# A pair's outputs turned one unit later, and the gate of the modulation made in an earlier phase

## The chip, the cores and the metric

The kernel runs on one core of a Trainium2 chip. The metric is the device time of one execution in microseconds (us); before the change its median is 1662.65 us over three runs. TensorE does the matrix products and the transposes, VectorE (DVE in the rows) and ScalarE (ACT) the elementwise work, GpSimd (POOL) small helpers and some transfers, and SyncE (SP) issues most loads. [...]

## The reference

One block of a hybrid network on 256 tokens `x` and 256 context tokens `ctx` of width 2048, in float32. What matters here:

```python
mod = jax.nn.silu(c) @ w_ada[l] + b_ada[l]            # 2048 -> 3 * 2048
shift, scale, gate = jnp.split(mod[:, None, :], 3, axis=-1)
xn = rmsnorm(h, norm_gain[l]) * (1.0 + scale) + shift  # cn: the context, with c_ctx
aq, ak, av, ag, hq, hff, hfb, hi, hg, ma, mb = split_columns(xn @ w_in[l])
caq, cak, cav, cag, chq, chff, chfb, chi, chg, cma, cmb = split_columns(cn @ w_in[l])
# window attention with rotary positions and a sink, over tokens and context -> att_branch
# f = lb + (1 - lb) * sigmoid(z): a scan in both directions over 16 heads of 128, its start
# state from the context -> o; o is normalised and gated -> hg_branch
y = sigmoid(ma + b[0]) * (hg_branch @ w_o_hgrn) + sigmoid(mb + b[1]) * (att_branch @ w_o_attn)
h = h + gate * (y @ w_out)
return rmsnorm(h, final_norm_gain)
```

`shift` and `scale` are needed at the very start. `gate`, the last third of the modulation (a row vector of 2048 values from a 2048 x 2048 piece of `w_ada`), is needed only at the very end.

## The kernel before

A float32 product is made of three products of split halves: each chunk of weights (128 x 1024) is loaded into a buffer `raw` (a rotation of four), ScalarE rounds it to the high half `wh` (L76, L577), and VectorE takes the difference as the low half `wl` (L77, L578). `wh` and `wl` have three buffers each. The stages in order of time, by the span of the profiled execution:

- To about 130 us: `x` and `ctx` are turned and normalised, `shift` and `scale` are made, and the first products with `w_in` run.
- To about 560 us: the forget gates and values of the scan, by a scheme with seven block products in place of eight (`quad_col`, 13 calls of seven steps; `quad_tok`, three calls of twice seven steps). VectorE also makes the weights' sums and differences (`combos`, L558). `bank8` deals out all eight PSUM banks in turn, among them those named `tp` and `o`. Results go to DRAM from the buffers F0.
- To about 1083 us: eight pairs of heads (`pair`), each a generator with small work on all engines. `weave` mixes it with a filler (`inputs`): the remaining projections of `w_in`, in chunks. A pair yields the amount of filler that it wants next, in units (STEP) of 24 matmuls of 512 columns; a filler chunk is half a unit, or a whole one where four blocks of tokens are projected.
- From about 1100 us: the output products `part_a` with `w_o_hgrn`, the attention, `part_b` with `w_o_attn`, then `w_out` and the last norm.

TensorE's order within the seven-product phase and within the pairs is that of the program (`manual_schedule`); that of the other engines and queues, and of TensorE's work outside such blocks, is set by the framework's planner, which runs its own model of time when the program is built, takes what is ready, and prefers what has a raised priority (`high_priority`: the splits `wh` and `wl`, the `combos`), and else what comes first in the program.

A pair does, in order: the scans that make the decays `E` (L741, L742, L745, in the buffer X2, which also holds the former pair's score tiles AT and state S2), gated queries and keys (L749 to L756), `copies(1)`, then a half unit of filler. Then the former pair's outputs are turned: `done` holds its function `turned` (L964 transposes `ot`, which L956 wrote into `so`; L969 and L970 write bH and bL, read by `part_a`). After another half unit come the transposes `tw` of `E` (L875), copied by ScalarE to `wT` (L876), a unit of filler, and the first products `sb` (L886). The rest of the pair builds the scores by levels, and ends with the products `ob` (L944 to L946), which L952, L181, L182 and L956 normalise and gate into `so`. The last pair's outputs are turned after the loop.

The gate: `gate_chunk` loads 256 rows by 512 columns of `w_ada` into a `raw` buffer and accumulates them on VectorE, each row block scaled by its value of silu(c) (L194 the first, L196 the others), into `accT[:, 0, :]`. After eight chunks `gate_end` transposes the sums (L202, tile `tqg`, bank `tp`, or `o` for the third group), reduces them (L204) and adds the bias in `gcol` (L206). There are four groups, 32 chunks. In the end `gcol` is transposed (L1073), copied and stored to `gate_rows`. `gates` does this as a generator; `with_gates` advances it by one chunk for each three units of filler that the pairs take, and what is left runs after the loop, behind the last turning (33 calls of `next`, which cover whatever remains). `accT[:, 1, :]` serves the pairs as a slot for copies.

Of the kernel before, what the change touches and what calls it, by code (L numbers as in the profile page):

```python
# [14 lines left out]
P = 128  # L15
# [23 lines left out]
def block_kernel(ctx: ExitStack, tc: tile.TileContext, x, c, cx, c_ctx, w_ada, b_ada, norm_gain, w_in,  # L39
# [147 lines left out]

    def gate_chunk(acc, g, k0):

        wr = wload(w_ada, k0 * P, 2, (4096 + 512 * g,), 512)[1][:, 0]  # L190
        for j in range(2):
            cc = cg[:, k0 + j: k0 + j + 1]
            if k0 + j == 0:
                dve.tensor_scalar(acc, wr[:, j, :], cc, None, op0=ALU.mult)  # L194
            else:
                dve.scalar_tensor_tensor(acc, wr[:, j, :], cc, acc, op0=ALU.mult, op1=ALU.add)  # L196
# [306 lines left out]
    def pairs_of(a):  # L503
        return a.rearrange("p (a t) -> p a t", a=2)

    with pl("sp", reuse_waits="tile") as sp:
        S = sp.tile([P, 2, 4, 8, T], F32R, name="S")

# [72 lines left out]
        def quad_col(d, h0):  # L581

            co = (C_FF, C_FB)[d] + h0 * HD
            b = {n: wload(w_in, 1024 * (n[0] == "2"), 8, (co + HD * (n[1] == "2"),), HD)[0]
                 for n in ("11", "12", "22", "21")}
            m_ = [bank8()[:, :T] for _ in range(3)]
            into = {0: (0, True), 1: (1, True), 2: (0, False), 3: (1, False), 4: (0, False), 5: (2, True), 6: (0, False)}
            sg = [base.tile([P, 512], F32, tag="sm", name="sg", bufs=3) for _ in range(2)]
            snap = [None] * 2
            for (i, _, mv), src in zip(ORDER, combos(b)):  # L590
                h, lo = [a.rearrange("p (k c) -> p k c", k=8) for a in two(src)]
                z, fresh = into[i]
                for k in range(8):
                    mh, ml = mv(k)
                    o = m_[z] if len(mh.shape) == 2 else pairs_of(m_[z])
                    pe.matmul(o, h[:, k, :], mh, start=fresh and k == 0, stop=False, skip_group_check=True)  # L596
                    pe.matmul(o, h[:, k, :], ml, start=False, stop=False, skip_group_check=True)  # L597
                for k in range(8):
                    mh, ml = mv(k)
                    o = m_[z] if len(mh.shape) == 2 else pairs_of(m_[z])  # L600
                    pe.matmul(o, lo[:, k, :], mh, start=False, stop=k == 7,  # L601
                              skip_group_check=True)
                with tc.high_priority(2 * PRIO):
                    if i in (0, 1):
                        if i == 0:
                            snap[0] = base.tile([P, 512], F32, tag="bb", name="sn", bufs=2)
                        act.activation(snap[0][:, i * T: (i + 1) * T], m_[i], AF.Copy)
                    elif i == 2:
                        snap[1] = base.tile([P, 512], F32, tag="bb", name="sn", bufs=2)
                        act.activation(snap[1][:, :T], m_[0], AF.Copy)  # L610
                    elif i == 3:
                        dve.tensor_tensor(half(sg[1], 0), pairs_of(m_[1]), pairs_of(snap[1][:, :T]), op=ALU.add)
                    elif i == 4:
                        dve.tensor_tensor(half(sg[1], 1), pairs_of(m_[0]), pairs_of(snap[0][:, T:]), op=ALU.add)
                    elif i == 5:
                        dve.tensor_tensor(half(sg[0], 0), pairs_of(m_[2]), pairs_of(snap[0][:, :T]), op=ALU.add)
                    else:
                        act.activation(half(sg[0], 1), pairs_of(m_[0]), AF.Sigmoid)
                if i == 4:
                    act.activation(sg[1], sg[1], AF.Sigmoid)  # L620
                elif i == 5:
                    act.activation(half(sg[0], 0), half(sg[0], 0), AF.Sigmoid)
            F = fp.tile([P, 2, 512], F32, tag="F0", name="F0", bufs=2)
            for i in (1, 0):
                dve.tensor_scalar(F[:, i, :], sg[i], lbc[:, 2 + d, h0 + i: h0 + i + 1],
                                  lbc[:, d, h0 + i: h0 + i + 1], op0=ALU.mult, op1=ALU.add)
            nc.gpsimd.dma_start(F_dr[d][h0 // 2], F.rearrange("p i t -> p (i t)"))

        def quad_tok(col0, dst):

# [32 lines left out]
            for s in range(2):  # L663
                b = {n: wload(w_in, 1024 * (n[0] == "2") + 512 * s, 4, (col0 + T * (n[1] == "2"),), T)[0]
                     for n in ("11", "12", "22", "21")}
                for (i, _, st_), src in zip(ORDER, combos(b)):
# [11 lines left out]
                                      skip_group_check=True)  # L678
                    if s == 1:
                        done_with(i)  # L680
            for t in range(2):
                nc.gpsimd.dma_start(dst[t], out[t].rearrange("p a c -> p (a c)"))

        with tc.manual_schedule(engines={mybir.EngineType.PE}):
# [12 lines left out]
                        quad_col(d, 2 * n)  # L697
            for g in range(1, 4):
                quad_tok(C_HI + 512 * g, v_dr[g])

    biases = {}

# [16 lines left out]
    def pair(g, p, grp, F, banks_q):  # L719
# [142 lines left out]

        copies(1)
        yield 0.5

        for f in done:
            f()
        done[:] = []
        yield 0.5
        wT = X2[:, 1024:].rearrange("p (a s) -> p a s", a=8)  # L870
        for d in range(2):
            tw = ps.tile([P, 512], F32, tag=alt(), name="tw")
# [2 lines left out]
                    pe.transpose(tw[:, (2 * i + s) * P: (2 * i + s + 1) * P], E[:, d, i, s * P: (s + 1) * P], ident)  # L875
            act.activation(wT[:, 4 * d: 4 * d + 4, :], tw.rearrange("p (a b) -> p a b", a=4), AF.Copy)  # L876
        yield 1.0
        so = hp.tile([P, 2, 512], F32, tag="so", name="so")
        qslot[64] = so[:, 1]
        S = so[:, 0, :].rearrange("p (d h v) -> p d h v", d=2, h=2)  # L880
# [179 lines left out]
            rows = slice(8 + 2 * t, 10 + 2 * t)  # L1060
            split(XH[:, rows, :], XL[:, rows, :], bv[t].rearrange("p (r c) -> p r c", r=2))

    def gates():

        for g in range(4):
            for k0 in range(0, KT, 2):
                gate_chunk(accT[:, 0, :], g, k0)
                yield
            gate_end(accT[:, 0, :], g)
        yield  # L1070

        tg = ps.tile([P, 512], F32, tag="tp", name="tgr")
        pe.transpose(tg[:KT, :P], gcol, ident)  # L1073
        grow_ = base.tile([P, 512], F32, tag="sm", name="grow", bufs=3)
        act.activation(grow_[:KT, :P], tg[:KT, :P], AF.Copy)
        nc.gpsimd.dma_start(gate_rows, grow_[:KT, :P])
        while True:
            yield

    def load_forgets(n):  # L1080
        F = [fp.tile([P, 2, 512], F32, tag=f"F{d}", name=f"F{d}", bufs=2 - d) for d in range(2)]
        for d in (1, 0):
# [28 lines left out]
        else:  # L1111
            run(side)

    def with_gates(filler):

        for got in filler:
            count[0] += got
            if count[0] >= 3 * STEP:
                count[0] -= 3 * STEP
                next(gate)  # L1120
            yield got

    y = [None] * 4

    def merge_gate(bm, n, row, dst):
# [5 lines left out]
            act.activation(dst[:, t, :], dst[:, t, :], AF.Sigmoid)  # L1131

    with tc.manual_schedule(engines={mybir.EngineType.PE}):
        accT = fp.tile([P, 2, 512], F32, tag="acc", name="acc")
        gate, count = gates(), [0]
        grps = [[None] * 3 for _ in range(4)]
        res = [load_forgets(0), None]
        run(output_gate(0))
# [1 line left out]
        for n in range(8):  # L1140
            if n % 2 == 0:
                load_values(n // 2, grps[n // 2])
                load_gate(n // 2, grps[n // 2])
            nxt = [None] * 2
            weave(pair(n // 2, n % 2, grps[n // 2], *res), with_gates(inputs(n, nxt)))
            res = nxt
        for f in done:
            f()
        for _ in range(33):
            next(gate)  # L1150

    def b_st(kt, t):
        sl = slice(t * P, (t + 1) * P)
# [327 lines left out]
```

## Time and profile before

| | |
|---|---|
| median of three runs | 1662.65 us (1662.18 to 1662.74) |
| the profiled execution | 1667.8 us; its span, first to last instruction, 1666.0 us |
| TensorE products busy | 1599.0 us, 96% of the span |
| VectorE busy | 1142.8 us, 69% |
| ScalarE busy | 844.0 us, 51% |
| mean granted clock of TensorE | 0.984 |

The rows of the profile name the line of the kernel, the engine (PE is TensorE, PEld its weight loads), the operation, and the tiles it writes and reads. A number in square brackets is the engine's idle time just before the instruction, with what ended it. The column PEclk is the share of its full clock that TensorE was granted.

### The profile page before, as it was taken

What the parts mean: (1) busy time and instruction counts of PE and PEld (TensorE: products, weight loads), DVE (VectorE), ACT (ScalarE), POOL (GpSimd) and SP (SyncE); (2) the same over time, 40 slices, a digit from 0 to 9 for tenths busy, and PEclk for the clock granted to TensorE, in tenths of its full rate; (3) what the DMA queues carried; (4) which work ended last, traced back from release to release, by engine and by line L of the source; (5) the groups of instructions that cost most, each with busy time, mean ns of one, the idle gap of its engine ahead of it and who ended that gap; (6) DMA issues with size and microseconds to landing.
All of it is one profiled execution on the core that took longest, in us unless ns stands there. A gap on an engine that the chain in (4) does not pass through costs nothing.

```text
span 1666.0 us, 28103 instructions
## 1 busy us (share of the span) xinstructions
PE 1599.0 (96%) x11250; PEld 1379.5 (83%) x11250; DVE 1142.8 (69%) x1677; ACT 844.0 (51%) x1317; POOL 83.6 (5%) x183
## 2 busy tenths in 40 slices
PE   7999999999999998989989999969999999999998
PEld 4668999999999887877878877748888888888887
DVE  4449877777777667767777787465567777756664
ACT  3334444444433456635656655324457787744442
POOL 2000000000000100101110010000000000000000
PEclk9999999999999999999999999979999999999999
DMA  9995344444343675745756665366654444567662
GB/s 366 386 349 177 127 128 135 132 127 128 130 136 127 230 230 179 241 152 164 237 198 212 228 207 171 129 222 189 191 175 152 146 142 155 158 205 244 222 194 90
DMA packets 230019, 312.86 MB, mean 188 GB/s; under 512 B 10080, under 2 KB 145664, under 8 KB 228992
## 3 DMA queue, kind: packets, MB, share of 16 engines
q1 hardware_dynamic: 216800, 266.85, 49.4%
q0 software_dynamic: 12368, 43.11, 7.4%
q8 instruction: 88, 1.44, 0.3%
q10 hardware_dynamic: 720, 1.11, 0.2%
q14 instruction: 43, 0.35, 0.1%
HBM read 290.05 MB, written 20.98 MB: 187 GB/s over the span
## 4 chain that ended last, share of the span: by engine, by line
PE 84%; DVE 7%; DMA 4%; issue 2%; ACT 2%; POOL 0%; SPq 0%; POOLq 0%; DVEq 0%; ACTq 0%
PE pj L83 14%; PE pj L84 13%; PE pj L85 13%; PE pj L141 5%; DMA raw<-in_w_ada_dram 3%; PE pj L601 3%; PE pj L597 3%; PE pj L596 3%; PE pj L146 3%; PE pm L601 3%; PE pm L597 3%; PE pm L596 3%; PE pj L415 2%; DVE wl L77 2%; PE pa L311 2%
## 5 line engine op out<-in xcount | busy, mean ns | idle before, releaser
L77 DVE TENSOR_TENSOR wl<-raw,wh 128x1024 fp32r<-128x1024 f32 x308 | 375.5, 1222 | 187.4 <-ACT wh L76 187.1
L76 ACT ACTIVATE wh<-raw 128x1024 fp32r<-128x1024 f32 x308 | 325.0, 1057 | 312.0 <-PE pj L85 220.0
L83 PE MATMUL pj<-wh,xHL 128*128 128x512 f32 (+1 forms) x832 | 325.3, 396 | 0.0
L84 PE MATMUL pj<-wl,xHL 128*128 128x512 f32 (+1 forms) x832 | 323.7, 389 | 0.0
L85 PE MATMUL pj<-wh,xHL 128*128 128x512 f32 (+1 forms) x832 | 323.0, 388 | 0.0
L85 PEld LDWEIGHTS pj<-wh,xHL 128*128 128x128 f32 x832 | 158.1, 190 | 32.5
L83 PEld LDWEIGHTS pj<-wh,xHL 128*128 128x128 f32 x832 | 158.5, 191 | 30.8 <-ACT sg L211 0.4
L84 PEld LDWEIGHTS pj<-wl,xHL 128*128 128x128 f32 x832 | 158.4, 190 | 30.8 <-DVE wl L77 0.8
L141 PE MATMUL pj<-xHL,wh 128*128 128x512 f32 x512 | 180.9, 395 | 0.0
L146 PE MATMUL pj<-xHL,wl 128*128 128x256 f32 x512 | 140.7, 285 | 0.3 <-DVE wl L77 0.3
L577 ACT ACTIVATE wh<-raw 128x1024 fp32r<-128x1024 f32 x76 | 80.5, 1059 | 99.2 <-issue 24.7
L141 PEld LDWEIGHTS pj<-xHL,wh 128*128 128x128 f32 x512 | 95.0, 188 | 18.6
L578 DVE TENSOR_TENSOR wl<-raw,wh 128x1024 fp32r<-128x1024 f32 x76 | 92.8, 1221 | 25.7 <-ACT wh L577 25.5
L83 PE MATMUL pj<-wh,bH 128*128 128x512 f32 x256 | 92.3, 397 | 15.5 <-ACT wh L76 15.4
L84 PE MATMUL pj<-wl,bH 128*128 128x512 f32 x256 | 101.6, 397 | 0.5 <-DVE wl L77 0.4
L85 PE MATMUL pj<-wh,bL 128*128 128x512 f32 x256 | 100.6, 394 | 0.0
L146 PEld LDWEIGHTS pj<-xHL,wl 128*128 128x128 f32 x512 | 96.6, 189 | 3.2 <-DVE wl L77 0.7
L577 ACT ACTIVATE wh<-T 128x1024 fp32r<-128x1024 f32 x57 | 60.3, 1058 | 74.3 <-DVE T L558 22.8
L578 DVE TENSOR_TENSOR wl<-T,wh 128x1024 fp32r<-128x1024 f32 x57 | 69.6, 1220 | 17.6 <-ACT wh L577 17.6
L83 PEld LDWEIGHTS pj<-wh,bH 128*128 128x128 f32 x256 | 48.6, 191 | 26.7 <-ACT wh L76 15.8
L196 DVE SCALAR_TENSOR_TENSOR acc<-raw,cg,acc 128x512 f32<-128x512 f32 x60 | 44.9, 749 | 36.6 <-DMA raw<-in_w_ada_dram 35.9
L851 DVE TENSOR_TENSOR A<-A,X 128x512 f32<-128x512 f32 x96 | 62.0, 687 | 8.2 <-ACT so L781 2.4
(363 smaller groups left out, 3145.7 us busy)
## 6 DMA issues: line engine op xcount, KB each, us to landing
raw<-in_w_in_dram SPq DMA_DIRECT2D x300, 512.0 KB, 3.6
raw<-in_w_ada_dram SPq DMA_DIRECT2D x96, 512.0 KB, 7.8
raw<-in_w_o_hgrn_dram SPq DMA_DIRECT2D x32, 512.0 KB, 3.6
raw<-in_w_o_attn_dram SPq DMA_DIRECT2D x32, 512.0 KB, 4.0
F<-F POOLq DMA_DIRECT2D x29, 512.0 KB, 4.5
raw<-in_w_out_dram SPq DMA_DIRECT2D x28, 512.0 KB, 3.9
v<-vo POOLq DMA_DIRECT2D x8, 512.0 KB, 3.4
X<-in_x_dram SPq DMA_DIRECT2D x2, 1024.0 KB, 7.1
```

The costliest lines, as they stand in the source:

```text
L76: act.activation(h[:, :n], raw[:, :n], AF.Copy)
L77: dve.tensor_tensor(lo[:, :n], raw[:, :n], h[:, :n].bitcast(F32), op=ALU.subtract)
L83: pe.matmul(o, s[0], m[0], start=first, stop=False)
L84: pe.matmul(o, s[0], m[1], start=False, stop=False)
L85: pe.matmul(o, s[1], m[0], start=False, stop=last)
L141: pe.matmul(banks[i].rearrange("p (a t) -> p a t", a=2), h[:, j, cs_], xHL[:, :, kt, :T], start=kt == 0, stop=kt == KT - 1)
L146: pe.matmul(banks[i][:, :T], lo[:, j, cs_], xH[:, kt, :T], start=False, stop=False)
L577: act.activation(h, src, AF.Copy)
L578: dve.tensor_tensor(lo, src, h.bitcast(F32), op=ALU.subtract)
L596: pe.matmul(o, h[:, k, :], mh, start=fresh and k == 0, stop=False, skip_group_check=True)
L597: pe.matmul(o, h[:, k, :], ml, start=False, stop=False, skip_group_check=True)
L601: pe.matmul(o, lo[:, k, :], mh, start=False, stop=k == 7, skip_group_check=True)
```

## The change

In a pair, the former pair's outputs are turned after the transposes `tw` and a unit of filler that follows them, in place of before them. The gate's loads go to a tile of their own (`wg`, on the tag F1 of the pool `fp`, one buffer), `accT` and the generator are made ahead of the seven-product phase, and that phase advances the gate: two chunks after each `quad_col`, two after each half of a `quad_tok`, and the rest, if any, at its end. With these counts the four groups end after the 5th, the 9th and the 13th call of `quad_col` and after the second half of the second `quad_tok`, where the transpose of `gcol` follows at once. `with_gates` and the calls after the loop are gone.

```diff
--- before.py
+++ after.py
@@ -187,7 +187,9 @@
 
     def gate_chunk(acc, g, k0):
 
-        wr = wload(w_ada, k0 * P, 2, (4096 + 512 * g,), 512)[1][:, 0]
+        wr = fp.tile([P, 2, 512], F32, tag="F1", name="wg")
+        nc.sync.dma_start(wr, w_ada[k0 * P: (k0 + 2) * P, 4096 + 512 * g: 4608 + 512 * g]
+                          .rearrange("(k p) c -> p k c", p=P))
         for j in range(2):
             cc = cg[:, k0 + j: k0 + j + 1]
             if k0 + j == 0:
@@ -502,6 +504,24 @@
 
     def pairs_of(a):
         return a.rearrange("p (a t) -> p a t", a=2)
+
+    def gates():
+
+        for g in range(4):
+            for k0 in range(0, KT, 2):
+                gate_chunk(accT[:, 0, :], g, k0)
+                yield
+            gate_end(accT[:, 0, :], g)
+        yield
+
+        tg = ps.tile([P, 512], F32, tag="tp", name="tgr")
+        pe.transpose(tg[:KT, :P], gcol, ident)
+        grow_ = base.tile([P, 512], F32, tag="sm", name="grow", bufs=3)
+        act.activation(grow_[:KT, :P], tg[:KT, :P], AF.Copy)
+        nc.gpsimd.dma_start(gate_rows, grow_[:KT, :P])
+
+    accT = fp.tile([P, 2, 512], F32, tag="acc", name="acc")
+    gate = gates()
 
     with pl("sp", reuse_waits="tile") as sp:
         S = sp.tile([P, 2, 4, 8, T], F32R, name="S")
@@ -625,6 +645,7 @@
                 dve.tensor_scalar(F[:, i, :], sg[i], lbc[:, 2 + d, h0 + i: h0 + i + 1],
                                   lbc[:, d, h0 + i: h0 + i + 1], op0=ALU.mult, op1=ALU.add)
             nc.gpsimd.dma_start(F_dr[d][h0 // 2], F.rearrange("p i t -> p (i t)"))
+            take(gate, 2)
 
         def quad_tok(col0, dst):
 
@@ -678,6 +699,7 @@
                                       skip_group_check=True)
                     if s == 1:
                         done_with(i)
+                take(gate, 2)
             for t in range(2):
                 nc.gpsimd.dma_start(dst[t], out[t].rearrange("p a c -> p (a c)"))
 
@@ -697,6 +719,7 @@
                         quad_col(d, 2 * n)
             for g in range(1, 4):
                 quad_tok(C_HI + 512 * g, v_dr[g])
+            take(gate, 60)
 
     biases = {}
 
@@ -862,11 +885,6 @@
 
         copies(1)
         yield 0.5
-
-        for f in done:
-            f()
-        done[:] = []
-        yield 0.5
         wT = X2[:, 1024:].rearrange("p (a s) -> p a s", a=8)
         for d in range(2):
             tw = ps.tile([P, 512], F32, tag=alt(), name="tw")
@@ -875,6 +893,11 @@
                     pe.transpose(tw[:, (2 * i + s) * P: (2 * i + s + 1) * P], E[:, d, i, s * P: (s + 1) * P], ident)
             act.activation(wT[:, 4 * d: 4 * d + 4, :], tw.rearrange("p (a b) -> p a b", a=4), AF.Copy)
         yield 1.0
+
+        for f in done:
+            f()
+        done[:] = []
+        yield 0.5
         so = hp.tile([P, 2, 512], F32, tag="so", name="so")
         qslot[64] = so[:, 1]
         S = so[:, 0, :].rearrange("p (d h v) -> p d h v", d=2, h=2)
@@ -1060,23 +1083,6 @@
             rows = slice(8 + 2 * t, 10 + 2 * t)
             split(XH[:, rows, :], XL[:, rows, :], bv[t].rearrange("p (r c) -> p r c", r=2))
 
-    def gates():
-
-        for g in range(4):
-            for k0 in range(0, KT, 2):
-                gate_chunk(accT[:, 0, :], g, k0)
-                yield
-            gate_end(accT[:, 0, :], g)
-        yield
-
-        tg = ps.tile([P, 512], F32, tag="tp", name="tgr")
-        pe.transpose(tg[:KT, :P], gcol, ident)
-        grow_ = base.tile([P, 512], F32, tag="sm", name="grow", bufs=3)
-        act.activation(grow_[:KT, :P], tg[:KT, :P], AF.Copy)
-        nc.gpsimd.dma_start(gate_rows, grow_[:KT, :P])
-        while True:
-            yield
-
     def load_forgets(n):
         F = [fp.tile([P, 2, 512], F32, tag=f"F{d}", name=f"F{d}", bufs=2 - d) for d in range(2)]
         for d in (1, 0):
@@ -1111,15 +1117,6 @@
         else:
             run(side)
 
-    def with_gates(filler):
-
-        for got in filler:
-            count[0] += got
-            if count[0] >= 3 * STEP:
-                count[0] -= 3 * STEP
-                next(gate)
-            yield got
-
     y = [None] * 4
 
     def merge_gate(bm, n, row, dst):
@@ -1131,8 +1128,6 @@
             act.activation(dst[:, t, :], dst[:, t, :], AF.Sigmoid)
 
     with tc.manual_schedule(engines={mybir.EngineType.PE}):
-        accT = fp.tile([P, 2, 512], F32, tag="acc", name="acc")
-        gate, count = gates(), [0]
         grps = [[None] * 3 for _ in range(4)]
         res = [load_forgets(0), None]
         run(output_gate(0))
@@ -1142,12 +1137,10 @@
                 load_values(n // 2, grps[n // 2])
                 load_gate(n // 2, grps[n // 2])
             nxt = [None] * 2
-            weave(pair(n // 2, n % 2, grps[n // 2], *res), with_gates(inputs(n, nxt)))
+            weave(pair(n // 2, n % 2, grps[n // 2], *res), inputs(n, nxt))
             res = nxt
         for f in done:
             f()
-        for _ in range(33):
-            next(gate)
 
     def b_st(kt, t):
         sl = slice(t * P, (t + 1) * P)
```

## The prediction

> **What bounds the kernel now.** I read, in this order, the page's busy shares and its 40 slices, the waits of TensorE, the busy time by stretches, and the timelines around the longest stalls. First the waits of TensorE from 600 us on (columns: who waited for whom, total us, times, longest us), then three stretches (window, length, busy of TensorE, its weight loads, VectorE, ScalarE, GpSimd, then clock, DMA share, GB/s).
>
> ```profile
> PE to L964 <- DVE so L956: 23.4, 12, 5.0
> PE pj L83 <- ACT wh L76: 15.4, 1, 15.4
> PE tqg L202 <- DVE bL L970: 4.1, 2, 2.9
> ```
>
> ```profile
> 180.00:560.00 380.00, 380.00 (x3169) 380.00 (x3168) 285.99 (x294) 171.13 (x218) 12.99 (x28) 1.00 0.42 134
> 600.00:1083.20 483.20, 452.52 (x4231) 381.48 (x4229) 350.57 (x595) 272.44 (x520) 47.69 (x106) 0.98 0.59 194
> 1083.20:1107.30 24.10, 8.49 (x22) 6.01 (x23) 17.16 (x26) 4.61 (x6) 0.00 (x0) 0.50 0.68 235
> ```
>
> The stretches are the seven-product phase, the eight pairs, and the step from the pairs to the output products. In the first TensorE never stops and VectorE is busy 75%. In the pairs TensorE idles 30.7 us, in the third stretch 15.6 us of 24.1, and what it does there runs at half clock. So TensorE is the bound, and time is to be had only in its holes. The waits name them: the turning of a pair's outputs (L964), the first output product (L83), the gate's transposes (L202).
>
> **The end of the pairs.** TensorE, VectorE and SP's queue there:
>
> ```profile
> 1083.20 0.36 PE L964 MATMUL to<-cs,so 128*128 128x128 f32 x1 [3.14 <-DVE so L956]
> ```
>
> ```profile
> 1088.03 7.83 DVE L196 SCALAR_TENSOR_TENSOR acc<-raw,cg,acc 128x512 f32<-128x512 f32 x10
> ```
>
> ```profile
> 1094.31 4.21 SPq L66 DMA_DIRECT2D raw<-in_w_o_hgrn_dram  x3
> ```
>
> The gate's last chunks hold the `raw` buffers until VectorE has accumulated them one after another, so the first load of `w_o_hgrn` is issued only at 1094.31, and TensorE restarts at 1100.88, cold. The clock, as windows of TensorE alone:
>
> ```profile
> 789.81:793.23 3.42, 1.85 (x15) 1.00 0.56 181
> 905.87:909.29 3.42, 3.41 (x10) 0.50 0.04 8
> 1100.88:1107.26 6.38, 6.34 (x14) 0.50 0.69 235
> ```
>
> Without the gate here the buffers come free with the last projection's chunks and those loads go out before the pairs end. That returns the 15.4 us and 6.34 / 2 = 3.2 us of clock. The 3.14 us ahead of the last turning I count as gone too: the output products are not in the hand-written order of the pairs (they start at 1100.88, before the last gate transposes, which are read only at 1107.99, a row below), they want heads 0 to 13 first, and with weights at hand they can run in that hole. If they don't, 3.1 us stay, and 1.7 us of clock. Sum 21.7, ends 17 and 22.
>
> **The pair boundaries.** TensorE's order there is now: at least one filler chunk, the turning of the old pair (it needs `so`, L956), filler, the transposes `tw` of the new pair's decays `E` (they need L745), filler. The change puts `tw` first and the turning a unit of filler behind it. TensorE at four of the seven boundaries, and the end of `E` on VectorE at three:
>
> ```profile
> 655.57 0.33 PE L964 MATMUL to<-cs,so 128*128 128x128 f32 x1 [2.67 <-DVE so L956]
> ...
> 720.23 0.99 PE L964 MATMUL to<-cs,so 128*128 128x128 f32 x2 [5.03 <-DVE so L956]
> ...
> 905.36 0.33 PE L964 MATMUL to<-cs,so 128*128 128x128 f32 x1 [2.04 <-DVE so L956]
> ...
> 964.03 0.48 PE L964 MATMUL to<-cs,so 128*128 128x128 f32 x1 [2.38 <-DVE so L956]
> ```
>
> ```profile
> 653.38 1.27 DVE L745 SCALAR_TENSOR_TENSOR X<-F,X 128x512 f32<-128x512 f32 x2
> ...
> 714.03 0.75 DVE L196 SCALAR_TENSOR_TENSOR acc<-raw,cg,acc 128x512 f32<-128x512 f32 x1 [3.51 <-DMA raw<-in_w_ada_dram]
> ...
> 961.51 1.26 DVE L745 SCALAR_TENSOR_TENSOR X<-F,X 128x512 f32<-128x512 f32 x2
> ```
>
> The wait is not simply removed: `E` lies in the buffer X2, which the old pair's last products read, so its scans start late too. TensorE reaches the place (start minus wait) at 652.90 in the first row and 961.65 in the last, and `E` ends at 654.65 and 962.77: `tw` would wait 1.75 and 1.12 us. These are the first and the last of four such boundaries; the two between give 2.78 and 1.13 by the same subtraction, in all 6.8 us. At 720.23 the scans stood behind a gate accumulate that waited 3.51 us for its load; without it `E` is ready before TensorE's arrival at 715.20. One later boundary has the same pattern, and one had no wait. So the pairs' 20.1 us at L964 (23.4 less 3.3 at the end) become 6.8: gain 13.3, ends 0 (`tw` inherits all) and 20.1. The turning then comes more than 5 us after `so` is done; the filler between covers it, and its results bH and bL are read only by the output products, so nobody waits for them.
>
> Each of these stalls also halves the clock for one or two windows of 3.41 us. The sum over the six such windows of the boundaries:
>
> ```profile
> sum 23.90, PE 21.50; mean PE 3.58
> ```
>
> 21.50 us of work at half clock are 10.75 us lost. A wait of 2.04 us ahead of 905.87 was enough; one of 2.9 us at 789.81 (the longest at L202), split over two windows, left the clock at 1.00. New waits of 1.1 to 1.8 us should mostly pass, the one of 2.78 may not: I keep 1.7 us of loss, gain 9.0. [...]
>
> The waits for the gate's transposes, 4.1 us, leave the pairs too. Gain in all 21.7 + 13.3 + 9.0 + 4.1 = 48.1 us.
>
> **What the gate costs in its new place.** Its 32 loads, 64 accumulates, 16 transposes with four reductions, and the last transpose, copy and store all move. The loads leave the rotation of `raw` and stand in SP's queue with a buffer of their own, F1, of one copy: each waits for the accumulates of the one before. VectorE's rows for the accumulator:
>
> ```profile
> L196 DVE SCALAR_TENSOR_TENSOR acc<-raw,cg,acc x60: 724/751/754, 602.2 to 1102.0; 128x512 f32<-128x512 f32 x60
> L194 DVE TENSOR_SCALAR acc<-raw,cg x4: 477/477/486, 600.6 to 1086.1; 128x512 f32<-128x512 f32 x4
> its engine sat idle before it (us, times) until:
>   DMA raw<-in_w_ada_dram: 37.2, 19
> ```
>
> VectorE gets 60 x 0.751 + 4 x 0.477 = 47.0 us of work, and may wait for loads as now, 37.2 us. Its idle time in the phase is 380 - 286 = 94 us. Two things hide this: that idle time, and VectorE's lead over TensorE. A low half of weights is ready at 309.49 and first used at 314.54, 5 us later:
>
> ```profile
> 308.27 1.22 DVE L578 TENSOR_TENSOR wl<-raw,wh 128x1024 fp32r<-128x1024 f32 x1
> ...
> 314.54 0.28 PE L601 MATMUL pm<-xHL,wl 128*128 128x256 f32 x1
> ```
>
> The last step of each of the 13 column products, for their pace:
>
> ```profile
> L618 ACT ACTIVATE sg<-pj x7: 384/384/384, 197.6 to 419.4; 128x256 f32<-128x256 f32 x7
> L618 ACT ACTIVATE sg<-pm x6: 384/384/384, 237.9 to 439.5; 128x256 f32<-128x256 f32 x6
> ```
>
> (439.5 - 197.6) / 12 = 20.2 us each. A quarter of the gate ends every four of them, 80.6 us: VectorE has 24.7% of that idle, 19.9 us, and needs 47.0 / 4 + 37.2 / 4 = 21.0 us. The overrun is 1.1 us a quarter, 4.4 us in all. Ends: 0 (the lead takes it) and 37.2 (no wait is absorbed). I take 4.4, near the bottom, since VectorE's idle time exceeds the need over the whole phase.
>
> On TensorE the order is fixed. The first group of transposes takes bank `tp` right behind a product that ScalarE must still read (0.384 us and two hand-overs): 0.6 us. The last group and the transpose of `gcol` follow each other with nothing between. Now:
>
> ```profile
> 1107.99 0.69 DVE L204 TENSOR_REDUCE redg<-tqg 128x4 f32<-128x512 f32 x1 [2.97 <-PE tqg L202]
> 1108.60 1.21 DVE L77 TENSOR_TENSOR wl<-raw,wh 128x1024 fp32r<-128x1024 f32 x1
> 1109.73 0.15 DVE L206 TENSOR_TENSOR gcol<-redg,gcol 128x4 f32<-128x4 f32 x1
> ```
>
> From the transposes to `gcol` that is 1.9 us; an addition that must first free the bank, taken like the reduction and perhaps behind a `wl`, makes it 3.3 us, and I add 0.9 us for an even chance of a half-clock window. The middle groups stand clear of their banks. In all 5 us, ends 2.5 and 8. The 16 transposes' own time is only moved.
>
> Sum: 48.1 - 5.0 - 4.4 = 38.7 us. The profiled execution took 1667.8 us (span 1666.0), 5.2 above the median of 1662.65; taken off the median, 1624 us.
>
> **Rivals.**
> - `tw` inherits the waits in full and no clock returns: 1662.65 - (21.7 + 4.1 - 9.4) = 1646 us. For it: `E` ends only 0.9 and 1.3 us before the turning's starts at 655.57 and 964.03. Against it: VectorE has no gate loads to wait for there any more.
> - VectorE's queue crowds the products: half to all of 37.2 us reaches TensorE, 1638 to 1657 us. Against it stand the 5 us of lead; for it, how such a wait looks now:
>
> ```profile
> 640.79 0.75 DVE L196 SCALAR_TENSOR_TENSOR acc<-raw,cg,acc 128x512 f32<-128x512 f32 x1 [4.35 <-DMA raw<-in_w_ada_dram]
> ...
> 645.60 1.23 DVE L77 TENSOR_TENSOR wl<-raw,wh 128x1024 fp32r<-128x1024 f32 x1 [3.20 <-ACT wh L76]
> ```
>
>   VectorE stood for 4.35 us, and the next split of weights came 5 us later. [...]
> - Slower, by SP's queue: a gate load that waits for F1 stands ahead of product weights. If every chunk held them by the mean wait, 37.2 / 19 = 1.96 us, 32 chunks lose 62.7 us: 1662.65 - 48.1 + 5 + 62.7 = 1682 us. It decides from 43.1 / 32 = 1.35 us a chunk on. Against it: TensorE has no wait at all in that phase now.
> - The gate is not made in time: accumulates planned late make each of the four transpose groups wait 2.9 us as at L202 now, and halve the clock (1.7): 18 us, 1642 us. Against it: VectorE's 94 us of idle time hold the 84 us of work and waits.
>
> **Chances.** Forecast (1611 to 1635) 0.62; `tw` 0.10; crowding 0.12; gate late 0.07; no change 0.03; SP's queue 0.06. A change under 0.2% (3.3 us) could not be told from none. Faster 0.91, same 0.03, slower 0.06. The low end has nothing lost on VectorE, 2.5 us at the transposes, `tw` waits of 1.1 us and the full clock, 1613 us, and 2 us to spare. The high end takes in the 1642 and 1646 cases and most of the crowding: 1650.
>
> **What would show it.** Right: no wait at L83 after the pairs, loads of `w_o_hgrn` issued before they end; waits at `tw` of 1 to 3 us instead of those at L964; full clock in the pairs but for a window or two; VectorE over 85% busy in the seven-product phase and TensorE still full. Wrong: waits of TensorE for `wl` or `wh` in that phase that add up to more than 10 us, or `tw` waiting at every boundary.

## The result and the profile after

The changed kernel takes 1622.11 us (1620.59 to 1623.79, four runs) against 1662.41 us of the kernel before (1659.75 to 1662.74, four runs): ratio 0.976, 95% interval 0.974 to 0.978. The profiled execution took 1623.79 us, its span 1622.0.

First the same two stretches as before the change, the seven-product phase and the pairs, up to where the output products now begin (columns as in the prediction):

```profile
180.00:560.00 380.00, 369.69 (x3016) 367.79 (x3017) 311.11 (x346) 164.16 (x211) 14.10 (x22) 0.98 0.52 166
...
600.00:1058.20 458.20, 455.88 (x4306) 386.99 (x4305) 330.44 (x552) 284.14 (x528) 46.59 (x104) 1.00 0.58 189
```

The pairs lost their holes: 2.3 us of idle time are left of 46.3 (30.7 in the pairs and 15.6 in the step behind them), and the clock is full. The seven-product phase, in which TensorE never stopped, now has 10.3 us of holes and a mean clock of 0.98. The waits of TensorE name both (who waited for whom, total us, times, longest us). `pj` and `pm` are the sums of products that TensorE builds, `sg` is the sum that VectorE makes of them at the end of a column product (called the column sum below), `tqg` and `tgr` are the gate's transposes:

```profile
PE pj L616 <- ACT wh L597: 3.0, 2, 2.2
PE tw L893 <- DVE X L768: 2.3, 4, 0.6
PE pj L697 <- DVE wl L598: 1.9, 1, 1.9
...
PE tgr L518 <- DVE gcol L208: 1.4, 1, 1.4
PE pj L621 <- DVE wl L598: 1.3, 1, 1.3
PE pj L616 <- DVE sg L634: 1.3, 2, 0.7
...
PE tqg L204 <- DVE vo L657: 0.8, 1, 0.8
PE tqg L204 <- ACT sg L638: 0.5, 1, 0.5
```

Of the pairs' waits only `tw` is left, 0.58 us at each of four boundaries; all other rows lie in the seven-product phase. There is no wait of the first output product (L83) and none at the turning. SP's queue and TensorE at the end of the pairs show why:

```profile
1041.65 22.32 SPq L66 DMA_DIRECT2D raw<-in_w_o_hgrn_dram  x5
```

```profile
1058.24 0.48 PE L83 MATMUL pj<-wh,bH 128*128 128x512 f32 x1
```

The loads of `w_o_hgrn` go out from 1041.65 on, and the first output product runs at 1058.24, before the last pair's outputs are turned (1074).

The half-clock windows of the seven-product phase, and how much TensorE worked in them:

```profile
186.89:190.31 3.42, 2.82 (x13) 2.82 (x14) 3.08 (x4) 2.45 (x3) 0.00 (x0) 0.50 0.14 27
190.31:193.72 3.41, 3.41 (x18) 3.41 (x18) 3.41 (x4) 1.44 (x2) 0.00 (x0) 0.50 0.78 250
500.92:504.33 3.41, 3.41 (x18) 3.41 (x17) 2.53 (x3) 0.76 (x1) 0.00 (x0) 0.50 0.65 197
538.47:541.88 3.41, 3.41 (x17) 3.41 (x18) 2.45 (x2) 0.45 (x2) 0.51 (x1) 0.50 0.20 72
sum 13.65, PE 13.05 PEld 13.05 DVE 11.47 ACT 5.10 POOL 0.51; mean PE 3.26 PEld 3.26 DVE 2.87 ACT 1.27 POOL 0.13
```

13.05 us at a granted clock of 0.50 are put at 6.5 us lost, the half. By the starts of products of 256 columns, every 0.21 us in the second of these windows and every 0.12 us behind it, it would be about 5.7. With the 10.3 us of holes the new place of the gate costs 16.8 us. Where the worst of it comes from is seen on VectorE:

```profile
147.37 0.49 DVE L196 TENSOR_SCALAR acc<-wg,cg 128x512 f32<-128x512 f32 x1 [1.22 <-DMA wg<-in_w_ada_dram]
147.77 1.22 DVE L77 TENSOR_TENSOR wl<-raw,wh 128x1024 fp32r<-128x1024 f32 x1
148.91 0.75 DVE L198 SCALAR_TENSOR_TENSOR acc<-wg,cg,acc 128x512 f32<-128x512 f32 x1
```

```profile
178.13 1.22 DVE L578 TENSOR_TENSOR T<-raw 128x1024 f32<-128x1024 f32 x1
...
181.00 0.74 DVE L198 SCALAR_TENSOR_TENSOR acc<-wg,cg,acc 128x512 f32<-128x512 f32 x1
181.66 1.22 DVE L578 TENSOR_TENSOR raw<-raw 128x1024 f32<-128x1024 f32 x1
182.80 1.22 DVE L598 TENSOR_TENSOR wl<-T,wh 128x1024 fp32r<-128x1024 f32 x1
...
185.07 1.22 DVE L578 TENSOR_TENSOR T<-raw,T 128x1024 f32<-128x1024 f32 x1
```

The same step as the last of these rows, in the kernel before:

```profile
177.67 1.21 DVE L558 TENSOR_TENSOR T<-raw,T 128x1024 f32<-128x1024 f32 x1
```

The program advances the gate first after the first column product, which ends near 205 us. The planner, free on every engine but TensorE, issued the first load at 142 and put the first accumulate at 147.37, among the token sums (L548), where VectorE has little room (busy 42.90 of the 47.00 us from 147 to 194 in the kernel before). Accumulates in two stretches (busy of VectorE in L198 alone):

```profile
147.00:194.00 47.00, 8.98 (x12) 0.93 0.53 165
194.00:286.00 92.00, 2.25 (x3) 1.00 0.47 145
```

With the one of L196, 13 of the first group's 16 are done by 194, before the call that the program puts them behind has ended. TensorE's holes there end at 180.55, 184.07 and 187.49, and each ends soon after a row above: the high half of the `T` of 178.13 is the first, the low half `wl` of 182.80 the second, the high half of the `T` of 185.07 the third. That last `T` comes 7.4 us later than in the kernel before, and ten accumulates, 7.2 us of VectorE's work, stand ahead of it in the queue.

### The profile page after: what moved, and what is told of

The parts are those of the page before. It is cut to its first block, busy times and chain, and to the rows that moved or that the text cites. A ratio compares the mean times of both kernels' runs of the same rounds, so it can differ in the third digit from the quotient of the medians.

```text
span 1622.0 us, 28104 instructions
## 1 busy us (share of the span) xinstructions
PE 1590.2 (98%) x11250; PEld 1374.7 (85%) x11250; DVE 1139.1 (70%) x1677; ACT 843.3 (52%) x1317; POOL 87.5 (5%) x183
## 4 chain that ended last, share of the span: by engine, by line
PE 78%; issue 10%; DVE 6%; DMA 4%; ACT 1%; POOL 0%; POOLq 0%; DVEq 0%; ACTq 0%; SPq 0%
PE pj L83 14%; PE pj L85 14%; PE pj L84 14%; PE pj L141 7%; PE pj L146 4%; DMA wg<-in_w_ada_dram 2%; PE pm L616 2%; PE pm L617 2%; PE pm L621 2%; PE pj L616 2%; PE pj L617 2%; PE pj L621 2%; DMA raw<-in_w_in_dram 2%; DVE wl L598 1%; PE al L828 1%
## 5 line engine op out<-in xcount | busy, mean ns | idle before, releaser
L83 PE MATMUL pj<-wh,xHL 128*128 128x512 f32 (+1 forms) x832 | 322.0, 392 | 0.0
L85 PEld LDWEIGHTS pj<-wh,xHL 128*128 128x128 f32 x832 | 156.3, 188 | 32.0
L83 PEld LDWEIGHTS pj<-wh,xHL 128*128 128x128 f32 x832 | 156.3, 188 | 30.1 <-ACT sg L213 0.4
L83 PE MATMUL pj<-wh,bH 128*128 128x512 f32 x256 | 91.8, 392 | 0.1
L84 PEld LDWEIGHTS pj<-wl,bH 128*128 128x128 f32 x256 | 48.1, 188 | 10.9 <-DVE wl L77 1.0
L83 PEld LDWEIGHTS pj<-wh,bH 128*128 128x128 f32 x256 | 47.8, 188 | 10.6 <-ACT bH L1067 0.5
```

The costliest lines, as they stand in the source:

```text
L83: pe.matmul(o, s[0], m[0], start=first, stop=False)
L84: pe.matmul(o, s[0], m[1], start=False, stop=False)
L85: pe.matmul(o, s[1], m[0], start=False, stop=last)
```

## Experiments

Lengths of five stages in the profiled executions, in us. The marks are TensorE's first product with a token sum `S` in the column products, and the first of the token products, of the pairs (`sb`), of the output products with bH, and of the last stage's `tky`.

| kernel | column | token, up to `sb` | pairs | output, attention | column + token |
|---|---|---|---|---|---|
| before | 259.2 | 166.2 | 495.4 | 400.3 | 425.4 |
| after | 270.6 | 174.1 | 433.0 | 399.2 | 444.7 |
| after, run again | 271.4 | 170.7 | 433.1 | 399.1 | 442.1 |
| turning alone | 259.2 | 165.8 | 474.9 | 399.2 | 425.0 |
| gate alone | 270.3 | 170.4 | 443.6 | 399.2 | 440.7 |
| no gate | 259.2 | 167.1 | 433.4 | 399.5 | 426.3 |
| start held | 266.0 | 171.7 | 432.9 | 399.2 | 437.7 |
| start held, last chunks earlier | 268.6 | 168.0 | 432.9 | 399.1 | 436.6 |
| paced | 266.2 | 173.3 | 433.1 | 399.2 | 439.5 |
| no buffer of its own | 268.9 | 173.2 | 432.9 | 399.2 | 442.1 |
| one column | 263.5 | 168.7 | 433.2 | 399.2 | 432.2 |
| three edits | 263.8 | 168.7 | 429.3 | 399.3 | 432.5 |

**The turning alone.** The kernel before with the pairs' edit only.

```diff
-        for f in done:
-            f()
-        done[:] = []
-        yield 0.5
         wT = X2[:, 1024:].rearrange("p (a s) -> p a s", a=8)
...
         yield 1.0
+        for f in done:
+            f()
+        done[:] = []
+        yield 0.5
```

> The kernel before with one part of the change alone: the old pair's outputs are turned after the transposes of the new pair's decays; the gate stays in the pairs. Theory A, the two parts lean on each other: the new transposes wait for the decays, and with the gate still on VectorE two boundaries keep 4.4 us each behind gate loads. Boundary waits then go from 20.1 to about 15.7 us, half of the lost clock returns (5 us), the 15.4 us ahead of the output products stay: about 1652 us (against 1662.4). Theory B, the parts are independent: the boundaries win the whole 17.8 us of waits and 10.8 us of clock that the changed kernel shows: about 1634 us.

Measured 1647.0 us (1642.88 to 1648.45), ratio 0.989 (0.987 to 0.991), between the two theories. TensorE's waits:

```profile
PE pj L83 <- ACT wh L76: 14.7, 1, 14.7
PE tw L870 <- DVE X L745: 10.8, 8, 2.5
...
PE to L964 <- DVE so L956: 3.3, 2, 3.1
```

The end keeps its waits, so those go with the gate's move. `tw` inherits 10.8 us, not 2.3, since here the gate still stands among the scans on VectorE:

```profile
1002.73 0.75 DVE L196 SCALAR_TENSOR_TENSOR acc<-raw,cg,acc 128x512 f32<-128x512 f32 x1 [2.22 <-DMA raw<-in_w_ada_dram]
...
1005.74 0.73 DVE L196 SCALAR_TENSOR_TENSOR acc<-raw,cg,acc 128x512 f32<-128x512 f32 x1
1006.39 0.69 DVE L745 SCALAR_TENSOR_TENSOR X<-F,X 128x512 f32<-128x512 f32 x1
...
1008.62 0.68 DVE L745 SCALAR_TENSOR_TENSOR X<-F,X 128x512 f32<-128x512 f32 x1
```

An accumulate that waits 2.22 us for its load stands ahead of the scans, another ahead of `E`, and `E`'s second half ends at 1009.30. At this boundary `tw` waits 2.10 and 1.58 us; with both parts it does not wait there at all. At 712 and 834 us an accumulate that waited for its load (2.32 and 1.51 us) stands ahead of the scans too, and `tw` waits 2.30 and 2.49 us; at 890 and 945 us, where none does, it waits the same 0.58 us as in the changed kernel (at 652 us, 1.18).

**The gate alone.** All of the change but the pairs' edit (the turning again ahead of `tw`).

> The changed kernel with the turning put back where it was: only the gate is moved. Both theories take away the 15.4 us, the 3.1 us and the 3.2 us of clock at the end of the pairs and the 4.1 us at the gate's transposes, and pay about 17 us in the seven-product phase. Theory A (the gate loads made two of the boundaries long): the boundary waits drop from 20.1 to about 13 us too, about 1646 us, and the gains of the two parts alone add up to some 15 us less than the 40 us of both. Theory B (independent parts): the boundaries stay at 20 us and their clock stays lost, about 1651 us.

Measured 1634.64 us (1630.4 to 1637.59), ratio 0.982 (0.980 to 0.984), better than both theories. The end's waits are gone, and the turnings (L987) wait 9.2 us at four boundaries in place of 20.1 at six. Pairs: 51.8 us shorter with the gate's move alone, 20.5 with the turning alone, 62.4 with both. The parts overlap by 9.9 us, because each shortens the same waits: the gate's move takes work and load waits out of VectorE's queue ahead of `so` and `E`, and the later turning gives them time. The 10.6 us of the turning behind the gate's move are its own worth here.

**No gate.** The changed kernel without the 32 loads, the 64 accumulates and the four groups' transposes and reductions.

```diff
-                gate_chunk(accT[:, 0, :], g, k0)
                 yield
-            gate_end(accT[:, 0, :], g)
```

> The changed kernel with the 32 loads, the 64 accumulates and the four groups' transposes and reductions left out (the gate is then the bias alone); the last transpose and its store stay. It prices the gate in its new place. Theory A, all of TensorE's 10.5 us of waits between 180 and 540 us and the half-clock windows behind them (6.8, 3.4 and 3.4 us) come from the gate: about 17 us less than the changed kernel, 1605 us. Theory B, part of these holes belongs to the phase itself and shows only now: at most 8 us less, 1614 us or more. Theory C, the gate also slows what its holes do not show (the pairs start later or with less lead): under 1600 us.

Measured 1615.82 us (1615.53 to 1615.99), ratio 0.971 (0.969 to 0.972). The time alone misleads: its modulation at the start took 10 us longer than in the others (last section). Column and token products together take 426.3 us against 444.7 and 442.1 in two executions of the changed kernel, so the gate costs 16 to 18 us there, near theory A; 2.6 of it are the transposes' own time that left the pairs (four groups of 0.66 us).

**The start held.** The first gate load waits for the first column product: GpSimd copies one of its results (a column of `F`) into the load's buffer first.

```diff
         wr = fp.tile([P, 2, 512], F32, tag="F1", name="wg")
+        if g + k0 == 0:
+            pool.tensor_copy(wr[:, 0, 0:1], late[0])
...
             nc.gpsimd.dma_start(F_dr[d][h0 // 2], F.rearrange("p i t -> p (i t)"))
+            late.append(F[:, 0, 0:1])
             take(gate, 2)
```

> The changed kernel with the gate's first load held until the first column product has given its result (a small copy on GpSimd writes one column of the buffer from that result, ahead of the load). Theory A, the holes at 180 to 188 us (4.3 us of waits, then 6.8 us at half clock) come from gate work that ran ahead into the token sums, where VectorE has no idle time: they go, about 7.5 us less, 1614.5 us. Theory B, any first eight chunks done in a burst use up VectorE's lead: the same holes come again some 20 us later, 1622 us.

Measured 1616.51 us (1614.92 to 1617.57), ratio 0.971 (0.970 to 0.973). The holes at 180 to 188 us and their half clock are gone, so the run-ahead was their cause. That is theory A. TensorE waits 4.0 us for the column sum here (at L618), against 1.7 in the first execution of the changed kernel; but in the second one (the last two rows, L616) it waits 3.8, so these runs do not show that the hold only moves part of the cost:

```profile
PE pj L618 <- DVE sg L636: 2.5, 3, 1.3
...
PE pm L618 <- DVE sg L636: 1.5, 1, 1.5
```

```profile
PE pj L616 <- DVE sg L634: 3.2, 3, 1.2
...
PE pm L616 <- DVE sg L634: 0.6, 1, 0.6
```

**The last chunks earlier too.** On top of that, the gate's chunks are taken in the order below in the token products, so that the last group's reduction is long over when the phase ends.

```diff
...
-            quad_tok(C_HI + 512 * g, v_dr[g])
+            quad_tok(C_HI + 512 * g, v_dr[g], ((2, 2), (2, 0), (1, 1))[g - 1])
```

> The held start, and the gate's last group moved two half products later: its transposes stand inside the third token product, where the bank tp is not in use, and the transpose of the result stands after that product. Theory A, the two holes behind the second token product (0.78 and 1.36 us with the held start) come from the bank that is still being read and from the two steps standing together: both go, 2 us less than the held start, 0.970 of the kernel before becoming 0.9697, 1612 us where the kernel before takes 1662.4. Theory B, the second wait (reduction and addition on VectorE) only moves: under 1 us less.

Measured 1613.86 us (1612.12 to 1615.3), ratio 0.969 (0.967 to 0.971). The waits of 0.78 us (`tqg`) and 1.36 us (`tgr`) are gone, as theory A has it. The times alone do not tell this kernel from the one with the held start: their ratios' intervals overlap. The waits for the column sum are 5.1 us in this execution, up to 2.48 us each, with one window of half clock.

**Paced.** Every pair of chunks held by the `F` of the column product ahead, not the first alone.

```diff
+        if late:
+            pool.tensor_copy(wr[:, 0, 0:1], late.pop())
...
+            late[:] = [F[:, 0, 0:1]]
             take(gate, 2)
```

> The changed kernel with every pair of gate chunks held until the column product ahead of it has given its result (the small copy on GpSimd before the first chunk of each pair), so that the chunks no longer come in bursts of eight. Theory A, TensorE's waits of 0.4 to 1.5 us for VectorE's additions at the column products (four of them, 3.8 us with only the start held) come from bursts: they go, about 11 us less than the changed kernel, 1611 us where the kernel before takes 1662.4. Theory B, each single late load costs, burst or not: as the held start, 1614.5 us, or longer where the pace is now set by the hold.

Measured 1618.12 us (1615.67 to 1619.3), ratio 0.972 (0.970 to 0.974), no better than one hold. The accumulates are spread as the program asks, and the waits for the column sum are spread with them (seven of 0.2 to 1.1 us): theory B, bursts are not what costs in the middle of the phase.

**No buffer of its own.** The gate's loads back in the rotation of `raw`.

```diff
-        wr = fp.tile([P, 2, 512], F32, tag="F1", name="wg")
-        nc.sync.dma_start(wr, w_ada[...].rearrange("(k p) c -> p k c", p=P))
+        wr = wload(w_ada, k0 * P, 2, (4096 + 512 * g,), 512)[1][:, 0]
```

> The changed kernel with the gate's loads in the rotation of the four raw buffers, as before the change, in place of a buffer of their own; the accumulates stay in the seven-product phase. Theory A, the own buffer is needed: each chunk takes a slot from the product weights, of which only four are in flight, and they come late: 0.5 us or more of TensorE for each of 32 chunks, 1638 us or more. Theory B, the buffer does not matter: about 1622 us; somewhat less is possible, since the rotation also keeps the gate from running ahead into the token sums (up to 7.5 us less, 1614.5 us).

Measured 1621.92 us (1618.35 to 1624.69), ratio 0.974 (0.972 to 0.976), against 0.976 (0.974 to 0.978) of the change. Theory B: the buffer is worth nothing that these runs could tell. The pairs take 432.9 us here, so their gain comes from the place of the gate's work, not from the buffer that its loads use. The seven-product phase has as many holes:

```profile
180.00:560.00 380.00, 369.25 (x3044) 366.76 (x3043) 310.77 (x349) 161.98 (x211) 11.76 (x21) 1.00 0.55 171
```

**One column.** Each accumulate does one column of 512, everything else stays, loads and waits too (the gate is mostly left out).

```diff
...
-                dve.scalar_tensor_tensor(acc, wr[:, j, :], cc, acc, op0=ALU.mult, op1=ALU.add)
+                dve.scalar_tensor_tensor(acc[:, :1], wr[:, j, :1], cc, acc[:, :1], op0=ALU.mult, op1=ALU.add)
...
```

> The changed kernel with all 32 gate loads, but accumulates of one column in place of 512 (the gate is then mostly left out); transposes and reductions stay. It tells VectorE's work from its waits and from SP's queue. Theory A, the holes come from 47 us of added work where VectorE is full: without it the start's 4.3 us with its clock, the waits for additions (1.7 us) and the 1.9 us in the token products go; what stays is some 3 us at the transposes: about 1609 us where the kernel before takes 1662.4. Theory B, the holes come from VectorE standing behind late loads, or from SP's queue: the loads are as late as before, the holes stay, 1618 us or more.

Measured 1612.98 us (1610.93 to 1616.99), ratio 0.969 (0.967 to 0.972). The accumulates, and VectorE's waits for their loads, in this kernel and then in the changed one:

```profile
L198 DVE SCALAR_TENSOR_TENSOR acc<-wg,cg,acc x60: 209/219/222, 149.9 to 486.1; 128x1 f32<-128x1 f32 x60
...
  DMA wg<-in_w_ada_dram: 14.1, 16
```

```profile
L198 DVE SCALAR_TENSOR_TENSOR acc<-wg,cg,acc x60: 741/749/757, 148.9 to 507.0; 128x512 f32<-128x512 f32 x60
...
  DMA wg<-in_w_ada_dram: 13.9, 17
```

VectorE stands as long for loads as before, 14.1 us, and yet most holes go: column and token products take 432.2 us, 10 to 12.5 less than in the changed kernel. That is theory A: without the work of the accumulates the same waits, and the same loads in SP's queue, cost little. The reverse, the full work with no late load, was not run. Over the kernel with no gate 5.9 us remain, 2.6 of them the transposes. A wait of 1.2 to 1.9 us for `wl` in the token products (between 477 and 500 us), which stands in every run with the full accumulates in this phase, is gone here.

**Three edits.** The held start, the last chunks earlier, and `tw` half a unit of filler later. The turning, of which the expectation speaks, keeps its place: half a unit less stands between it and `tw`. The changed kernel was run again beside it.

```diff
         copies(1)
-        yield 0.5
+        yield 1.0
         wT = X2[:, 1024:].rearrange("p (a s) -> p a s", a=8)
...
-        yield 1.0
+        yield 0.5
         for f in done:
```

> The changed kernel with the gate's first load held until the first column product has its sum, the last chunks taken earlier among the token products, and the turn of the outputs half a unit later still (yield 1.0 before it and 0.5 behind it). Theory A (the four waits of tw for X that are left, 0.58 us each, 2.3 us, end when the scans' product X has had another half unit, and nothing takes their place): the output stage falls from 433.0 to about 430.7 us, no wait at the turn, and the time is about 2.3 us under that of the kernel held in the same two places, ratio to the kernel before about 0.968. Theory B (the turn then comes within reach of the next boundary, and o waits for its column sum or the products for the turned tiles): a new wait of 0.5 to 2 us at some of the turns or all of them, output stage 433 to 445 us, ratio 0.970 to 0.977.

> The changed kernel as it is, on the same chip as the kernel with the three further edits. Theory A (the holes at the phase's two ends and their windows of half clock are a property of the program's order): the same holes as in its first profile, 180 to 188 us and 536 to 539 us, ratio 0.974 to 0.978, and 8 to 11 us behind the kernel with the three edits. Theory B (they came of that one execution or chip): other holes, and less than 5 us between the two.

Measured 1607.57 us (1607.48 to 1609.15), ratio 0.966 (0.964 to 0.969), against 1620.71 us (1617.49 to 1621.32), ratio 0.973 (0.971 to 0.976): 13.1 us apart on one chip. It is the fastest version of this study. `tw` no longer waits (theory A), and TensorE is busy in every microsecond of 600 to 1040. First this kernel's two stretches, then the seven-product phase of the changed kernel run again, with its one window of half clock there:

```profile
180.00:560.00 380.00, 375.55 (x3125) 374.60 (x3124) 319.37 (x358) 167.43 (x214) 11.76 (x23) 1.00 0.55 174
600.00:1040.00 440.00, 440.00 (x4223) 374.82 (x4222) 321.72 (x543) 274.85 (x518) 44.85 (x101) 1.00 0.59 190
```

```profile
180.00:560.00 380.00, 368.55 (x3042) 366.32 (x3042) 312.14 (x347) 164.62 (x212) 11.79 (x22) 1.00 0.52 165
186.78:190.19 3.41, 2.98 (x14) 2.98 (x15) 3.16 (x4) 2.28 (x3) 0.00 (x0) 0.50 0.15 29
```

The holes at both ends of the phase stand at the same places again: they belong to the program's order. That is theory A too, though the second hole, with waits of 0.8 and 1.4 us as in the first execution, costs no half clock this time, and the ratio of 0.973 and the 13.1 us lie just outside what the theory named. This execution lost 11.5 us in holes and 1.5 to the clock, 13.0 in all, against 16.8 in the first. The pairs (the output stage of the expectation) gained 3.6 us, of which the four waits are 2.3; where the other 1.3 come from was not separated. The column products are also 4.8 us shorter than with the holds alone, with the same edits to that phase: the waits for the column sum (2.2 us here, 5.1 there) and one half-clock window differ between these executions. Whether that is a mere difference of executions stays open.

## Why the prediction was right, and where it was not

1624 us was forecast, 1622.11 measured. The order of events was as forecast. The gains came out 10.9 us larger than forecast and the costs 7.4 us larger, and these nearly cancel: that the sum came within 2 us is luck.

- **End of the pairs, 21.7 us: right.** All three parts came back, and with the turning alone 14.7 of the 15.4 us, the 3.1 us and the half clock stay.
- **Boundaries, 13.3 us: too small.** Of 20.1 us at the turning 2.3 remained, not 6.8: a gain of 17.8. The step that failed is the subtraction, in two ways. It took the end of the second half of `E`, but the first transposes need the first half alone, as these rows of the changed kernel show:

```profile
669.81 1.27 DVE L768 SCALAR_TENSOR_TENSOR X<-F,X 128x512 f32<-128x512 f32 x2
```

```profile
670.53 1.26 PE L893 MATMUL tw<-cs,X 128*128 128x128 f32 x8 [0.58 <-DVE X L768]
```

  The two rows at L768, one for each half, end at 671.08 together, and `tw` starts at 670.53, when only the first has ended. With the turning alone, the gate still in the pairs, the four boundaries of the subtraction show 1.18, 2.49, 0.58 and 0.58 us where it had 1.75, 2.78, 1.13 and 1.12. And it read the scans from a trace in which the gate's work still stood on VectorE, and cleared that at one boundary only: with the gate out of the pairs the four are 0.58 us each.
- **Clock in the pairs, 9.0 us: 10.75**, half of the 21.50 us at a clock of 0.50. No window of half clock remained; 1.7 us had been kept for one behind a wait of 2.78 us that did not come.
- **Gate transposes, 4.1 us: right**, and waits of 3.0 us that I had left out (at L946 and L927) went as well.
- **The gate's ends on TensorE, 5.0 us: 4.4 measured.** Waits of 0.5, 0.8 and 1.4 us and 1.7 us of clock at 538.47, which the prediction had as 0.6, 3.3 and 0.9 (in sum 4.8, taken as 5.0).
- **VectorE's crowding, 4.4 us: the mis-sized term.** The rest of 16.8 us is 12.4 us in the first execution and about 10.3 in the second (13.0 less 2.7 of the same three waits, with no half clock at 538). The working spread the work evenly over four groups of 80.6 us and let TensorE's lead take the rest. In fact the planner began it at 147 us, in the token sums, and even when spread as the program asks it delays the column sum. VectorE's waits for the gate's loads, put at 37.2 us, measured 15.1 (13.9 and 1.2); with them the working gives no overrun at all, 62.1 / 4 = 15.5 us of 19.9, so the working had no ground for the cost that came. The bound, that VectorE's idle time exceeds the need, held (82% busy); it does not bound a wait, because what stands behind an accumulate is not always early. The rival "crowding" described the place rightly, but its mechanism, waits for loads, does not do it alone: with one column the loads still make VectorE wait 14.1 us, and most holes are gone.

The signs that the text named: no wait at L83, loads issued before the pairs end, full clock in the pairs: seen. `tw` waits of 1 to 3 us: 0.58 each. VectorE over 85% busy and TensorE still full: neither, 82% and 10.3 us of holes. More than 10 us of waits for `wl` or `wh`: about 6, the rest at the column sum and the gate's ends.

In sum the two stretches lost 61.3 us before (46.3 idle, 10.75 and 4.2 of clock, the last half of 8.49 us of products in the step behind the pairs) and 2.3 after, a gain of 59.0 for 48.1 forecast; the cost was 16.8 for 9.4. The difference, 42.2, was forecast as 38.7, where the medians stand 40.3 apart and the two profiled executions 44.0.

## What to carry to other kernels

Filler work belongs where the bound engine does not wait on the engine that does it, and its lateness is read per queue, not from the idle share of a phase. Where a planner orders an engine, the place of a call in the program does not hold its work back: only a dependency does, and one small copy that ties the first load to the right event removed 4.3 us of holes and 3.1 us of lost clock at the start of the phase here (ratio 0.971, against 0.976 and 0.973 in two sets of runs of the changed kernel). Two edits that shorten the same waits don't add up, so a part's worth depends on which comes first.

## What the runs showed of the hardware

**A wait cost a window of half clock or none, by where it fell.** In the trace of the kernel before and in that of the changed one, the places at which the granted clock changes (15 and 9 of them) lie whole multiples of 3.413 us apart. Two boundaries of the kernel with the gate alone, each with the window that holds the wait and the one behind it:

```profile
899.24:902.65 3.41, 1.44 (x7) 0.86 (x5) 3.41 (x8) 2.29 (x4) 1.55 (x2) 1.00 0.37 132
902.65:906.07 3.42, 3.30 (x9) 2.54 (x10) 3.42 (x9) 0.47 (x1) 0.00 (x0) 0.50 0.04 8
957.27:960.68 3.41, 1.63 (x8) 1.01 (x6) 3.41 (x7) 2.47 (x5) 1.58 (x3) 1.00 0.81 293
960.68:964.09 3.41, 2.62 (x13) 2.03 (x14) 3.41 (x8) 0.47 (x1) 0.62 (x1) 1.00 0.14 19
```

At the first boundary 1.97 and 0.12 us are idle, nearly all of it in one window, and the next window is at half clock. At the second there is more, 1.78 and 0.79 us, but it lies across two windows, and the clock stays. In the traces of the kernel before (40 to 1655 us) and of the changed one (40 to 1612 us), ten full-clock windows of this grid were followed by half clock; they had 1.89 to 3.14 us of idle time. All others were followed by full clock; they had 1.57 us at most. Short waits counted together: 0.78 and 1.37 us, 2.15 in one window, came ahead of the one at 538.47. The ten half-clock windows that were followed by full clock had 0.17 us of idle time at most, the eight that were not 0.49 to 3.42. So in these traces the length of a wait alone does not tell what it cost. How the clock is decided they do not show.

**The same DMA traffic ran at two rates.** In the modulation the kernel without the gate moved less than the changed one, from the same program up to there (same columns):

```profile
40.00:110.00 70.00, 63.41 (x354) 37.59 (x347) 29.59 (x73) 20.95 (x37) 0.00 (x0) 1.00 1.09 352
```

```profile
40.00:110.00 70.00, 70.00 (x390) 42.77 (x391) 31.67 (x79) 23.95 (x42) 0.00 (x0) 1.00 1.08 386
```

352 against 386 GB/s, at DMA shares of 1.09 and 1.08; it cost 10 us, in a kernel whose four runs lie within 0.5 us. The profiles of all other kernels have the higher rate, three from the same chip among them. The cause was not found, and what else ran on the chip then is not on record.
